# Attention's softmax, query splits and PSUM copies at the scheduler's highest priority, the copies on VectorE, in a hybrid trunk

## The chip, the core and the metric

The kernel runs on one core of a Trainium2 chip. The core has a matrix engine (TensorE, PE in the profile), a vector engine (VectorE, DVE), a scalar engine for functions of one variable (ScalarE, ACT), GpSimd (POOL) and a queue engine from which most transfers are issued (SyncE, SP). Each has its own list of instructions. The metric is the device time of one execution in microseconds (us); of the kernel before there are three, and their median counts.

## The reference: what is computed

Two layers over x (1024 tokens, width 1024, float32). The core of a layer:

```
h    = rms_norm(x, pre_gain) * (1 + scale) + shift      # shift, scale, gate from SiLU(c) @ W_mod + b_mod
proj = h @ w_in                                         # 3088 columns, split among three branches
a_out = sliding_window_attention(rotary(aq), rotary(ak), av, sinks) * silu(ag)
r_out = rms_norm(retention(rq, rk, rv)) * silu(rg)
g_out = rms_norm(gated_linear_attention(gq, gk, gv, log_a)) * silu(gg)
y    = concat(a_out, r_out, g_out) @ w_out
x    = x + gate * rms_norm(y, post_gain)
```

The attention has 8 query heads of width 64 over 2 key/value heads and a window of 128 tokens: token i sees the 128 tokens that end with itself. A learned number for each head, the sink, joins the softmax as one more score and has no value behind it. The three branches have nothing to do with each other until the output projection joins them.

## The kernel before, in words

**Tiles and stages.** The 1024 tokens make 8 tiles of 128. All matrix products of float32 numbers are done in three passes with each operand split into a high and a low part (`PASSES`), so nearly every operand gets a copy (the high part, often on ACT) and a subtraction (the low part, often on DVE). A layer first does the gate paths, retention and the gated linear attention (0 to 340 us and 480 to 820 us of the profiled span), and then attention, which overlaps with the rest of the input projection, the output projection's weights and, in layer 0, the modulation of the next layer (340 to 480 us and 820 to 965 us). The output projection follows.

**What sets the order.** The program is emitted by generators: `job` puts one on a list, `pump` advances all that are due. A generator yields how long the next step should come after (the table `L`, by a planning clock `clk` that counts the matmuls emitted) or a flag for which it waits. PE executes its instructions in exactly the order in which they are emitted, since its order is set by hand (`manual_schedule` for PE). The order of the other engines' instructions is made by a scheduler, by priority among those that can go; unless something else is said, priority is the order of emission. `tc.high_priority()` gives the instructions inside it the highest priority. In the finished program each engine works through its list strictly in order, so that an instruction that waits holds up all that stand behind it. Which engine does an elementwise step is said by the table `EN` ("A" is ACT, "V" DVE, "G" POOL, "S" SP); the helpers `copy` (L150 on ACT, L152 on DVE), `eng`, `dma` (L155), `mult` (L166, matmuls) and `transp` (L181) look there, and so most of the work has the helpers' lines in the profile.

**Attention, tile by tile.** `attn_run` starts `attn_q(l, t)` for t from 0 to 7. For one tile:

1. The queries are split into high and low part by `attn_split` (ACT L912, DVE L913), usually by the tile before.
2. The tile `smx` gets the sink as its last column (DVE L921).
3. 24 matmuls (`aux<-kT,t`) put the scores of this and the previous block of keys into four PSUM banks of the pool `aux`.
4. For t > 0, four copies move the scores of the previous block to `smx` (ACT, `smx<-aux` at L150), and four masked copies put the scores of the own block over them where the mask is set (DVE L947). Since window and block have the same size, one 128x128 square holds both.
5. Softmax: maximum (DVE L949), eight exponentials with sums (ACT L952), reciprocal (DVE L955), product with it (POOL L957).
6. The square is transposed in blocks of 32 (DVE L959). Blocks on the diagonal hold scores of two key blocks; for these, `vd`, the difference of two values (POOL L964), and `pr`, the masked probabilities (POOL L968), are made.
7. The products with the values (`aux<-smx,vx` and those with `vd`) go to four banks `po` of the same pool.
8. **The copies of the change**: four copies of 128x128 bring the result out of PSUM into `ao` (L150, `t<-aux` 128x128; ACT). They are called `aoc0` and `aoc1` in `EN`. Over 2 layers and 8 tiles there are 64.
9. `ao` is stored to DRAM (`aoS<-t`, issued by SP), read back in another arrangement together with the gate (`t<-aoS`, `t<-gS`), multiplied (DVE L1003), split (L152, POOL L1010) and stored to `mixS`, from which `load_mix` reads `mx`, the input of the output projection. In layer 1 `load_mix` belongs to `last_output`.

**PSUM banks.** Of 8 banks, `mm` has three and `aux` five. Scores of a tile take four of `aux`, and so do the products with the values. With the order of PE as emitted, the scores of tile t + 2 go into the banks that the copies of tile t set free: the first score matmul finds one bank free, the second needs the first copy done. Scores of tile t + 2 stand behind the value products of tile t on PE. A buffer is freed when its last reader is done, whichever engine that is.

**Others that the steps touch.** L368 adds up the modulation of the next layer from weights that are being loaded (`st<-in_w_mod_dram`). L575 sums blocks of layer 1's output weights (`st<-in_w_last_dram`). L786 sets `gaT` to zero (POOL). L1276, L1342 and L1408 belong to the output projection. L844 is the low part of the keys. SP issues loads of weights, the stores and read-backs above in one list.

Of the kernel before, what the change touches and what calls it, by code (L numbers as in the profile page):

```python
# [94 lines left out]
def trunk(ctx: ExitStack, tc: tile.TileContext, ins, cst, out):  # L95
    nc = tc.nc
    V, A, G, T = nc.vector, nc.scalar, nc.gpsimd, nc.tensor
# [6 lines left out]
    gp = ctx.enter_context(tc.tile_pool(name="work", bufs=2))  # L104
# [18 lines left out]
    def small(w, dt=F32):  # L123
        return gp.tile([P, w], dt, tag="sm", name=nm("sm"), bufs=BS)
# [20 lines left out]
    def eng(k):  # L145
        return G if EN[k] == "G" else V

    def copy(k, dst, src):
        if EN[k] == "A":
            A.activation(dst, src, AF.Copy)  # L150
        else:
            V.tensor_copy(dst, src)  # L152

    def dma(k, dst, src):
        {"S": nc.sync, "A": A, "P": G}[EN[k]].dma_start(dst, src)  # L155

# [27 lines left out]
    def lat(key, l):  # L184

        return L[key + "@1"] if l and key + "@1" in L else L[key]
# [4 lines left out]
    def flag(name, lat=0.0):  # L191
        flags[name] = clk[0] + lat
# [465 lines left out]
    def pre(l, t, xt, early=False, soon=False):  # L658
# [28 lines left out]
        for j in range(2):  # L687
# [92 lines left out]
    kv = {}  # L780
# [31 lines left out]
    for l in range(DEPTH):  # L812
        c = slice(P * l, P * l + P)
# [93 lines left out]
            job(attn_q(l, t))  # L907

    def attn_split(t):
        qs = [t2(F32R).rearrange("p (k q) -> p k q", k=4) for _ in range(2)]  # L910
        qt = kv[t // 4][:, :, P * (t % 4):P * (t % 4) + P]
        A.activation(qs[0], qt, AF.Copy)  # L912
        eng("qsl").tensor_tensor(qs[1], qt, f(qs[0]), ALU.subtract)  # L913
        kv["qs"][t] = qs

    def attn_q(l, t):

        if t not in kv["qs"]:
            attn_split(t)
        sm = gp.tile([P, 8, 129], F32, tag="smx", name=nm("smx"), bufs=SMB)  # L920
# [16 lines left out]
        if t + 1 < NT and flags.get(("q", l, (t + 1) // 4, 1), 1e9) <= clk[0]:  # L937
            attn_split(t + 1)
        if t % 4 == 3:
            flag(("s", l, t // 4))  # L940
        for g in range(2):
            for r in range(2):
                pv = pss[g][r][:, 0:2 * n].rearrange("p (j c n) -> p j c n", j=2, n=P)
                sv = sm[:, 4 * g + r:4 * g + 4:2, 0:128]
                if t > 0:
                    copy("sprev", sv, pv[:, :, 0, :])
                V.copy_predicated(sv, curmask.unsqueeze(1).to_broadcast((P, 2, P)), pv[:, :, n // P - 1, :])  # L947
        mx = small(8)
        V.tensor_reduce(mx, sm, AX.X, ALU.max, negate=True)  # L949
        sums = small(8)  # L950
        for h in range(8):
            A.activation(sm[:, h, :], sm[:, h, :], AF.Exp, bias=mx[:, h:h + 1],  # L952
                         accum_out=sums[:, h:h + 1])
        rs = small(8)
        V.reciprocal(rs, sums)  # L955
        ph = sm[:, :, 0:128]
        eng("pn").tensor_tensor(ph, ph, rs.unsqueeze(2).to_broadcast((P, 8, P)), ALU.mult)  # L957
        pb = ph.rearrange("p h (j b) -> p h j b", j=4)
        V.transpose(pb, pb)  # L959
        cur, prev = kv[("v", t // 2)], kv.get(("v", max(t - 1, 0) // 2))  # L960
        tc_, tp = t % 2, (t - 1) % 2
        if t > 0:
            vd = gp.tile([P, P], F32, tag="vd", name=nm("vd"), bufs=2)
            G.tensor_tensor(vd, cur[:, 8 + tc_], prev[:, 8 + tp], ALU.subtract)  # L964
            pr = gp.tile([P, 8, 32], F32, tag="pr", name=nm("pr"), bufs=2)
            for i in range(4):
                rr = slice(32 * i, 32 * i + 32)
                eng(f"pr{i}").tensor_tensor(pr[rr], pb[rr, :, i, :], dmask[rr].unsqueeze(1).to_broadcast((32, 8, 32)),  # L968
                                            ALU.mult)
        yield lat("aq4", l)  # L970
        po = [aux() for _ in range(4)]
        for s in range(5 if t else 4):
            for i in range(4):
                rr = slice(32 * i, 32 * i + 32)
                j = (i + s) % 4
# [10 lines left out]
                    mult(d3, w_, x, s == 0, s == (4 if t else -i % 4 if i < 2 else 3), 0.03)  # L986
        ao = t2()
        av = ao.rearrange("p (h q) -> p h q", h=4)
        for i in range(4):
            copy(f"aoc{i % 2}", av[:, :, 32 * i:32 * i + 32], po[i][:, 0:128].rearrange("p (h a) -> p h a", h=4))  # L990
        flag(("av", l, t))
        dma("sao", aoS[t], av)
        if t in (2, 4):
# [5 lines left out]
        av = ao.rearrange("p (k q) -> p k q", k=4)  # L999
# [7 lines left out]
        if not whole or t % 2 == 0:  # L1007
            mh, ml = t2(F32R), t2(F32R)
# [706 lines left out]


B2, B1, BS, BST, MMB, SMB = 10, 8, 11, 5, 3, 3
EN = {"shw0": "V", "shw1": "A", "shw2": "A", "shw3": "A", "slw0": "V", "slw1": "G", "slw2": "V", "slw3": "G", "sht2": "A", "sht3": "A", "sht4": "A", "slt2": "V", "slt3": "G", "slt4": "G", "sd": "V", "mh0": "A", "mh1": "A", "mh2": "A", "mh3": "A", "mf": "A", "ms0": "V", "ms1": "V", "ms2": "V", "ms3": "V", "yg0": "V", "yg1": "V", "ml0": "V", "ml1": "V", "ml2": "V", "ml3": "V", "mod0": "A", "mod1": "V", "qst": "S", "sv": "S", "sg": "S", "lv": "S", "pr0": "G", "pr1": "G", "pr2": "G", "pr3": "G", "smh": "S", "sml": "S", "sm0": "S", "sm1": "S", "lao": "S", "sao": "S", "lmix": "S", "ssg": "S", "lsg": "S", "ssr": "S", "lsr": "S", "lx": "S", "sx": "A", "lw": "S", "lwm": "S", "whi0": "V", "whi1": "A", "whi2": "A", "whi3": "A", "wlo0": "V", "wlo1": "V", "wlo2": "V", "wlo3": "G", "xn0": "V", "xn1": "V", "hlo0": "V", "hlo1": "V", "rot0": "V", "rot1": "V", "rdec": "V", "kslo": "V", "qslo": "V", "vlo": "G", "kT": "A", "qT": "A", "sprev": "A", "pn": "G", "pf0": "A", "aoc0": "A", "aoc1": "A", "qsl": "V", "hng": "V", "mh": "A", "gso": "V", "mg": "V", "mgl": "G", "rT": "A", "rv": "A", "gv": "A", "gk": "A", "ak0": "V", "ak1": "V", "ak2": "V", "ak3": "V", "kd0": "G", "kd1": "G", "kd2": "G", "kx1": "G", "kx2": "G", "kx3": "V", "kx4": "V", "qb": "G", "stx": "V"}
# [44 lines left out]
```

## Time and profile before

| | |
|---|---|
| three executions | 1028.87, 1028.4, 1024.04 us; median 1028.4 |
| the profiled execution, its own time | 1027.32 us |
| its span in the trace | 1025.5 us |
| mean granted PE clock | 0.967 |
| chain that ended last, by engine | PE 65%, DVE 11%, DMA 9%, issue 6%, POOL 5%, ACT 2% |
| data moved by DMA | 163.59 MB, mean 160 GB/s |

How to read the rows. The page gives for each engine the busy time, the share of the span and the number of instructions; PEld is the loading of weights into PE, which runs beside the matmuls. A row of windows has the stretch in us and its length, then busy time and number of instructions of PE, PEld, DVE, ACT and POOL, the granted PE clock as a share of the full one, the busy share of the DMA engines and GB/s. A row of waits names the engine with its instruction, the instruction that ended the wait, and us in total, times and the longest. A row of groups names line, engine, operation, output<-inputs with shapes, the number of instructions, then busy us and mean ns of one, and the engine's idle time before them. A row of the timeline has the start, the duration of a run of like instructions, the engine and line, the number, and in brackets how long the engine was idle before and what ended that. "SPq" is an issue of a transfer by SP. PE's ends are modelled, and a few matmul records are missing (23 of 24 scores in some rows).

### The profile page before, as it was taken

The numbers are of one execution on the slowest core, as the hardware profiler recorded it, in microseconds if no ns is written. First come the engines' busy times: TensorE is split into PE (matmuls) and PEld (weight loads), VectorE is DVE, ScalarE is ACT, GpSimd is POOL, SyncE is SP. The second block draws the span as 40 slices with busy tenths as digits, with TensorE's granted clock in tenths as the row PEclk, the third lists the DMA queues.
The fourth block names the chain that finished last, engine by engine and source line by source line (L and its number), as shares of the span: only waits on it lengthen the run. The fifth ranks groups of instructions, "written<-read, shape, count | busy, mean of one in ns | idle before, by whom it ended". The sixth has DMA issues, their size and how long they took to land.

```text
span 1025.5 us, 21284 instructions
## 1 busy us (share of the span) xinstructions
PE 959.5 (94%) x7965; PEld 832.5 (81%) x7965; DVE 695.7 (68%) x1628; ACT 388.8 (38%) x1152; POOL 282.1 (28%) x319
## 2 busy tenths in 40 slices
PE   5899999999999996888999999999999999778896
PEld 1599999888989775666889999988998877566685
DVE  3789857678666877564388286775774686676776
ACT  2577312333313553412455332133332355454221
POOL 2322111233211355451124101123330044566000
PEclk8899999999999998898999999999999999879899
DMA  8843414433453447867545141351234334787883
GB/s 302 293 132 110 143 43 138 141 104 104 123 175 97 135 139 250 279 191 269 188 151 175 64 155 33 115 175 58 88 104 144 94 111 144 235 278 231 277 255 136
DMA packets 115528, 163.59 MB, mean 160 GB/s; under 512 B 13232, under 2 KB 56796, under 8 KB 115424
## 3 DMA queue, kind: packets, MB, share of 16 engines
q1 hardware_dynamic: 109728, 152.66, 46.9%
q10 hardware_dynamic: 5696, 9.56, 2.5%
q8 instruction: 63, 1.03, 0.4%
q14 instruction: 41, 0.34, 0.1%
HBM read 118.66 MB, written 41.42 MB: 156 GB/s over the span
## 4 chain that ended last, share of the span: by engine, by line
PE 65%; DVE 11%; DMA 9%; issue 6%; POOL 5%; ACT 2%; SPq 1%; ACTq 0%; POOLq 0%; DVEq 0%
PE mm L166 51%; PE aux L166 11%; PE aux L181 3%; DMA aoS<-t 2%; DMA st<-in_w_in_dram 2%; POOL sm L639 1%; DMA t<-gS 1%; POOL smx L957 1%; DMA xk<-in_x_dram 1%; DVE acc L368 1%; ACT smx L952 1%; SPq L155 1%; DMA mx<-mixS 1%; DVE arena L537 1%; POOL pr L968 1%
## 5 line engine op out<-in xcount | busy, mean ns | idle before, releaser
L166 PE MATMUL mm<-arena 128*128 128x256 f32 (+2 forms) x1824 | 296.6, 318 | 2.1 <-ACT arena L708 1.8
L166 PE MATMUL mm<-arena,arena 128*128 128x256 f32 (+2 forms) x1824 | 295.8, 317 | 0.0
L166 PEld LDWEIGHTS mm<-arena 128*128 128x128 f32 x1824 | 257.4, 192 | 24.9 <-ACT arena L708 2.0
L166 PEld LDWEIGHTS mm<-arena,arena 128*128 128x128 f32 x1824 | 254.1, 189 | 23.8 <-issue 2.2
L166 PE MATMUL mm<-arena,mx 128*128 128x512 f32 (+1 forms) x564 | 138.1, 402 | 11.1 <-DMA mx<-mixS 5.9
L639 POOL TENSOR_TENSOR sm<-sm,mhalf 128x1 f32<-128x1 f32 (+1 forms) x64 | 55.3, 864 | 322.5 <-DVE sm L638 309.4
L166 PEld LDWEIGHTS mm<-arena,mx 128*128 128x128 f32 x564 | 106.5, 198 | 37.0 <-issue 7.9
L150 ACT ACTIVATE arena<-st 128x512 fp32r<-128x512 f32 x94 | 55.8, 628 | 64.3 <-PE mm L166 27.0
L537 POOL TENSOR_TENSOR arena<-st,arena 128x512 fp32r<-128x512 f32 x31 | 44.0, 1422 | 120.6 <-ACT arena L150 116.8
L952 ACT ACTIVATE smx<-smx,sm 128x129 f32<-128x129 f32 x128 | 49.7, 390 | 54.6 <-DVE sm L949 54.6
L150 ACT ACTIVATE t<-aux 128x128 f32<-128x128 f32 (+3 forms) x124 | 38.2, 355 | 65.1 <-PE aux L181 63.2
L537 DVE TENSOR_TENSOR arena<-st,arena 128x512 fp32r<-128x512 f32 x77 | 58.1, 776 | 4.0 <-ACT arena L150 2.7
L368 DVE SCALAR_TENSOR_TENSOR acc<-st,c_act,acc 128x512 f32<-128x512 f32 x60 | 47.6, 793 | 16.0 <-DMA st<-in_w_mod_dram 15.4
L957 POOL TENSOR_TENSOR smx<-smx,sm 128x1024 f32<-128x1024 f32 x16 | 32.1, 2004 | 84.2 <-DVE sm L955 71.2
L181 PE MATMUL aux<-c_ident,t 128*128 128x128 f32 (+1 forms) x292 | 48.7, 285 | 6.5 <-DVE t L670 6.2
L968 POOL TENSOR_TENSOR pr<-smx,c_dmask 32x256 f32<-32x256 f32 x56 | 49.6, 886 | 17.1 <-DVE smx L921 7.2
L181 PEld LDWEIGHTS aux<-c_ident,t 128*128 128x128 f32 (+1 forms) x292 | 35.3, 145 | 14.2 <-DVE t L670 8.4
L166 PE MATMUL aux<-kT,t 64*128 64x256 f32 (+1 forms) x384 | 31.7, 308 | 13.9 <-ACT t L150 13.9
L166 PEld LDWEIGHTS aux<-kT,t 64*128 64x128 f32 x384 | 27.4, 205 | 20.1 <-ACT t L150 14.7
L702 ACT ACTIVATE t<-aux,mod,mod 128x128 f32<-128x128 f32 x68 | 25.9, 462 | 44.8 <-DVE t L1311 11.6
L166 PEld LDWEIGHTS aux<-t,mx 32*128 32x128 f32 (+1 forms) x896 | 39.5, 187 | 3.8 <-issue 2.2
L1036 ACT ACTIVATE t<-aux 128x256 f32<-128x256 f32 x32 | 12.3, 384 | 76.9 <-PE aux L166 69.8
(224 smaller groups left out, 1395.3 us busy)
## 6 DMA issues: line engine op xcount, KB each, us to landing
st<-in_w_in_dram SPq DMA_DIRECT2D x96, 256.0 KB, 4.0
st<-in_w_mod_dram SPq DMA_DIRECT2D x64, 256.0 KB, 3.0
mx<-mixS SPq DMA_DIRECT2D x20, 512.0 KB, 5.5
st<-in_w_last_dram SPq DMA_DIRECT2D x36, 256.0 KB, 3.3
mixS<-t SPq DMA_DIRECT2D x64, 128.0 KB, 1.9
mixS<-t SPq DMA_DIRECT2D x26, 256.0 KB, 3.2
wm<-in_w_mod_dram SPq DMA_DIRECT2D x12, 512.0 KB, 5.4
t<-in_x_dram SPq DMA_DIRECT2D x24, 256.0 KB, 4.5
```

The source lines that it names most:

```text
L150: A.activation(dst, src, AF.Copy)
L155: {"S": nc.sync, "A": A, "P": G}[EN[k]].dma_start(dst, src)
L166: T.matmul(dst, lhsT, rhs, start=start, stop=stop)
L181: T.transpose(dst, src, idn)
L368: V.scalar_tensor_tensor(acc, wt, c_act[:, k:k + 1], acc, ALU.mult, ALU.add)
L537: e.tensor_tensor(lo, st, f(hi), ALU.subtract)
L639: G.tensor_tensor(r, r, mhalf[:, :w], ALU.pow)
L702: A.activation(hf[:, ks], at[kt], AF.Identity, scale=gain, bias=shift)
L952: A.activation(sm[:, h, :], sm[:, h, :], AF.Exp, bias=mx[:, h:h + 1], accum_out=sums[:, h:h + 1])
L957: eng("pn").tensor_tensor(ph, ph, rs.unsqueeze(2).to_broadcast((P, 8, P)), ALU.mult)
L968: eng(f"pr{i}").tensor_tensor(pr[rr], pb[rr, :, i, :], dmask[rr].unsqueeze(1).to_broadcast((32, 8, 32)), ALU.mult)
L1036: A.activation(sq, po, AF.Square)
```

## The change

Three things are edited. (1) The softmax part of `attn_q`, from the copies of scores to `vd` and `pr` (steps 4 to 6), becomes a function `soft`, called under `tc.high_priority()`; it hands on `vd` and `pr` in `kv["m"]`. (2) The query split (step 1) and the four copies of step 8 are emitted under `tc.high_priority()` too. (3) These copies go from ACT to VectorE. The order on PE and what is computed stay the same; the sizes of pools and the latencies `L` are not touched. In the built program DVE has 1694 instructions in place of 1630, and ACT 940 in place of 1004.

```diff
     def attn_split(t):
-        qs = [t2(F32R).rearrange("p (k q) -> p k q", k=4) for _ in range(2)]
         qt = kv[t // 4][:, :, P * (t % 4):P * (t % 4) + P]
-        A.activation(qs[0], qt, AF.Copy)
-        eng("qsl").tensor_tensor(qs[1], qt, f(qs[0]), ALU.subtract)
+        with tc.high_priority():
+            qs = [t2(F32R).rearrange("p (k q) -> p k q", k=4) for _ in range(2)]
+            A.activation(qs[0], qt, AF.Copy)
+            eng("qsl").tensor_tensor(qs[1], qt, f(qs[0]), ALU.subtract)
         kv["qs"][t] = qs
+
+    def soft(t, n, pss, sm):
...
+        if t > 0:
+            vd = gp.tile([P, P], F32, tag="vd", name=nm("vd"), bufs=2)
+            G.tensor_tensor(vd, kv[("v", t // 2)][:, 8 + t % 2], kv[("v", (t - 1) // 2)][:, 8 + (t - 1) % 2],
+                            ALU.subtract)
...
+            kv["m"] = vd, pr
 
     def attn_q(l, t):
...
-        cur, prev = kv[("v", t // 2)], kv.get(("v", max(t - 1, 0) // 2))
+        with tc.high_priority():
+            soft(t, n, pss, sm)
+        pb = sm[:, :, 0:128].rearrange("p h (j b) -> p h j b", j=4)
+        cur, prev = kv[("v", t // 2)], kv[("v", max(t - 1, 0) // 2)]
         tc_, tp = t % 2, (t - 1) % 2
...
+        vd, pr = kv["m"] if t else (None, None)
         yield lat("aq4", l)
...
         av = ao.rearrange("p (h q) -> p h q", h=4)
-        for i in range(4):
-            copy(f"aoc{i % 2}", av[:, :, 32 * i:32 * i + 32], po[i][:, 0:128].rearrange("p (h a) -> p h a", h=4))
+        with tc.high_priority():
+            for i in range(4):
+                copy(f"aoc{i % 2}", av[:, :, 32 * i:32 * i + 32], po[i][:, 0:128].rearrange("p (h a) -> p h a", h=4))
...
-EN = { ... "aoc0": "A", "aoc1": "A", ... }
+EN = { ... "aoc0": "V", "aoc1": "V", ... }
```

The lines of `soft` that are left out are those of steps 4 to 6, unchanged in content and order.

More of the change, by code (lines that the diff above doesn't have):

```diff
@@ L909, in attn_split @@
     def attn_split(t):
-        qs = [t2(F32R).rearrange("p (k q) -> p k q", k=4) for _ in range(2)]
         qt = kv[t // 4][:, :, P * (t % 4):P * (t % 4) + P]
-        A.activation(qs[0], qt, AF.Copy)
-        eng("qsl").tensor_tensor(qs[1], qt, f(qs[0]), ALU.subtract)
+        with tc.high_priority():
+            qs = [t2(F32R).rearrange("p (k q) -> p k q", k=4) for _ in range(2)]
+            A.activation(qs[0], qt, AF.Copy)
+            eng("qsl").tensor_tensor(qs[1], qt, f(qs[0]), ALU.subtract)
         kv["qs"][t] = qs
+    def soft(t, n, pss, sm):
+        for g in range(2):
+            for r in range(2):
+                pv = pss[g][r][:, 0:2 * n].rearrange("p (j c n) -> p j c n", j=2, n=P)
+                sv = sm[:, 4 * g + r:4 * g + 4:2, 0:128]
+                if t > 0:
+                    copy("sprev", sv, pv[:, :, 0, :])
+                V.copy_predicated(sv, curmask.unsqueeze(1).to_broadcast((P, 2, P)), pv[:, :, n // P - 1, :])
+        mx = small(8)
+        V.tensor_reduce(mx, sm, AX.X, ALU.max, negate=True)
+        sums = small(8)
+        for h in range(8):
+            A.activation(sm[:, h, :], sm[:, h, :], AF.Exp, bias=mx[:, h:h + 1],
+                         accum_out=sums[:, h:h + 1])
+        rs = small(8)
+        V.reciprocal(rs, sums)
+        ph = sm[:, :, 0:128]
+        eng("pn").tensor_tensor(ph, ph, rs.unsqueeze(2).to_broadcast((P, 8, P)), ALU.mult)
+        pb = ph.rearrange("p h (j b) -> p h j b", j=4)
+        V.transpose(pb, pb)
+        if t > 0:
+            vd = gp.tile([P, P], F32, tag="vd", name=nm("vd"), bufs=2)
+            G.tensor_tensor(vd, kv[("v", t // 2)][:, 8 + t % 2], kv[("v", (t - 1) // 2)][:, 8 + (t - 1) % 2],
+                            ALU.subtract)
+            pr = gp.tile([P, 8, 32], F32, tag="pr", name=nm("pr"), bufs=2)
+            for i in range(4):
+                rr = slice(32 * i, 32 * i + 32)
+                eng(f"pr{i}").tensor_tensor(pr[rr], pb[rr, :, i, :], dmask[rr].unsqueeze(1).to_broadcast((32, 8, 32)),
+                                            ALU.mult)
+            kv["m"] = vd, pr
     def attn_q(l, t):
@@ L940, in attn_q @@
             flag(("s", l, t // 4))
[L941 to L959, printed above, removed]
-        cur, prev = kv[("v", t // 2)], kv.get(("v", max(t - 1, 0) // 2))
-        tc_, tp = t % 2, (t - 1) % 2
[L962 to L965, printed above, removed]
-            for i in range(4):
-                rr = slice(32 * i, 32 * i + 32)
-                eng(f"pr{i}").tensor_tensor(pr[rr], pb[rr, :, i, :], dmask[rr].unsqueeze(1).to_broadcast((32, 8, 32)),
-                                            ALU.mult)
+        with tc.high_priority():
+            soft(t, n, pss, sm)
+        pb = sm[:, :, 0:128].rearrange("p h (j b) -> p h j b", j=4)
+        cur, prev = kv[("v", t // 2)], kv[("v", max(t - 1, 0) // 2)]
+        tc_, tp = t % 2, (t - 1) % 2
+        vd, pr = kv["m"] if t else (None, None)
         yield lat("aq4", l)
@@ L988, in attn_q @@
         av = ao.rearrange("p (h q) -> p h q", h=4)
-        for i in range(4):
-            copy(f"aoc{i % 2}", av[:, :, 32 * i:32 * i + 32], po[i][:, 0:128].rearrange("p (h a) -> p h a", h=4))
+        with tc.high_priority():
+            for i in range(4):
+                copy(f"aoc{i % 2}", av[:, :, 32 * i:32 * i + 32], po[i][:, 0:128].rearrange("p (h a) -> p h a", h=4))
         flag(("av", l, t))
@@ L1717 @@
 B2, B1, BS, BST, MMB, SMB = 10, 8, 11, 5, 3, 3
-EN = {"shw0": "V", "shw1": "A", "shw2": "A", "shw3": "A", "slw0": "V", "slw1": "G", "slw2": "V", "slw3": "G", "sht2": "A", "sht3": "A", "sht4": "A", "slt2": "V", "slt3": "G", "slt4": "G", "sd": "V", "mh0": "A", "mh1": "A", "mh2": "A", "mh3": "A", "mf": "A", "ms0": "V", "ms1": "V", "ms2": "V", "ms3": "V", "yg0": "V", "yg1": "V", "ml0": "V", "ml1": "V", "ml2": "V", "ml3": "V", "mod0": "A", "mod1": "V", "qst": "S", "sv": "S", "sg": "S", "lv": "S", "pr0": "G", "pr1": "G", "pr2": "G", "pr3": "G", "smh": "S", "sml": "S", "sm0": "S", "sm1": "S", "lao": "S", "sao": "S", "lmix": "S", "ssg": "S", "lsg": "S", "ssr": "S", "lsr": "S", "lx": "S", "sx": "A", "lw": "S", "lwm": "S", "whi0": "V", "whi1": "A", "whi2": "A", "whi3": "A", "wlo0": "V", "wlo1": "V", "wlo2": "V", "wlo3": "G", "xn0": "V", "xn1": "V", "hlo0": "V", "hlo1": "V", "rot0": "V", "rot1": "V", "rdec": "V", "kslo": "V", "qslo": "V", "vlo": "G", "kT": "A", "qT": "A", "sprev": "A", "pn": "G", "pf0": "A", "aoc0": "A", "aoc1": "A", "qsl": "V", "hng": "V", "mh": "A", "gso": "V", "mg": "V", "mgl": "G", "rT": "A", "rv": "A", "gv": "A", "gk": "A", "ak0": "V", "ak1": "V", "ak2": "V", "ak3": "V", "kd0": "G", "kd1": "G", "kd2": "G", "kx1": "G", "kx2": "G", "kx3": "V", "kx4": "V", "qb": "G", "stx": "V"}
@@ new lines @@
+EN = {"shw0": "V", "shw1": "A", "shw2": "A", "shw3": "A", "slw0": "V", "slw1": "G", "slw2": "V", "slw3": "G", "sht2": "A", "sht3": "A", "sht4": "A", "slt2": "V", "slt3": "G", "slt4": "G", "sd": "V", "mh0": "A", "mh1": "A", "mh2": "A", "mh3": "A", "mf": "A", "ms0": "V", "ms1": "V", "ms2": "V", "ms3": "V", "yg0": "V", "yg1": "V", "ml0": "V", "ml1": "V", "ml2": "V", "ml3": "V", "mod0": "A", "mod1": "V", "qst": "S", "sv": "S", "sg": "S", "lv": "S", "pr0": "G", "pr1": "G", "pr2": "G", "pr3": "G", "smh": "S", "sml": "S", "sm0": "S", "sm1": "S", "lao": "S", "sao": "S", "lmix": "S", "ssg": "S", "lsg": "S", "ssr": "S", "lsr": "S", "lx": "S", "sx": "A", "lw": "S", "lwm": "S", "whi0": "V", "whi1": "A", "whi2": "A", "whi3": "A", "wlo0": "V", "wlo1": "V", "wlo2": "V", "wlo3": "G", "xn0": "V", "xn1": "V", "hlo0": "V", "hlo1": "V", "rot0": "V", "rot1": "V", "rdec": "V", "kslo": "V", "qslo": "V", "vlo": "G", "kT": "A", "qT": "A", "sprev": "A", "pn": "G", "pf0": "A", "aoc0": "V", "aoc1": "V", "qsl": "V", "hng": "V", "mh": "A", "gso": "V", "mg": "V", "mgl": "G", "rT": "A", "rv": "A", "gv": "A", "gk": "A", "ak0": "V", "ak1": "V", "ak2": "V", "ak3": "V", "kd0": "G", "kd1": "G", "kd2": "G", "kx1": "G", "kx2": "G", "kx3": "V", "kx4": "V", "qb": "G", "stx": "V"}
```

## The prediction

> **What bounds the kernel now.** I read the head of the page first, then busy time by stage, then PE's waits.
>
> ```profile
> span 1025.5 us, 21284 instructions
> PE 959.5 (94%) x7965; PEld 832.5 (81%) x7965; DVE 695.7 (68%) x1628; ACT 388.8 (38%) x1152; POOL 282.1 (28%) x319
> ```
> ```profile
> core 0: us, PE busy (x) PEld busy (x) DVE busy (x) ACT busy (x) POOL busy (x), PEclk, DMA share, GB/s
> 340.00:480.00 140.00, 120.91 (x1131) 95.09 (x1130) 89.75 (x140) 55.83 (x212) 62.50 (x57) 0.93 0.66 207
> 480.00:820.00 340.00, 337.60 (x2784) 309.92 (x2783) 219.21 (x605) 123.23 (x341) 66.06 (x89) 1.00 0.38 123
> 820.00:965.00 145.00, 125.25 (x1151) 98.41 (x1150) 101.33 (x153) 68.22 (x232) 72.92 (x63) 0.90 0.65 203
> 878.00:900.00 22.00, 16.12 (x141) 12.48 (x141) 14.51 (x22) 8.25 (x31) 10.85 (x11) 0.77 0.81 273
> ```
> ```profile
> PE aux L166 <- ACT t L150: 17.7, 7, 6.4
> PE aux L166 <- DVE smx L947: 10.5, 3, 5.3
> PE mm L166 <- DMA mx<-mixS: 5.9, 2, 5.2
> ```
> TensorE is busy for 94% of the span, and its instruction order is fixed by hand. The two attention stages (340 to 480 and 820 to 965 us) are the ones that the change touches. PE idles there for 19.1 and 19.8 us, in the middle of layer 1 for 2.4 us only. The attention waits are named: 17.7 us in 7 waits for the copies of values out of PSUM (ACT, L150), 10.5 us in 3 for softmax (L947). DVE is busy for 64% and 70% of these stages, ACT for 40% and 47%. So the change aims at a real wait, and moves the copies from the emptier engine to the fuller one. What decides is where in DVE's order they stand.
>
> **The change part by part.** *Price of the copies.*
>
> ```profile
> L150 ACT ACTIVATE t<-aux 128x128 f32<-128x128 f32 x64 | 12.8, 268 | 1.7 <-DVE t L1311 1.7
> L844 DVE TENSOR_TENSOR kT<-aux,kT 128x128 fp32r<-128x128 f32 x16 | 4.5, 282 | 0.5 <-ACT kT L843 0.2
> ```
> ```profile
> 354.47 1.43 DVE L947 COPY_PREDICATED smx<-c_curmask,aux 128x256 f32<-128x256 int32 x4
> ```
> ACT loses 64 copies of 268 ns (12.8 us, overlapped). DVE gains 64. No row shows a plain 128x128 copy on DVE; the nearest is L844, of the same size out of PSUM, at 282 ns: 18 us at most. Four in a row lie between ACT's own 0.74 us (row 360.78 below) and four masked copies of twice the size in 1.43; I take 0.8, nearer to the first. [...]
>
> *Priority.* In the built programs PE's order is the same. Softmax and splits move by few places on ACT, DVE and POOL (two swaps on POOL), since most stood as early as their inputs allow: I cost that at nothing beyond the places named below. What counts is that each engine executes in order, so the copies now wait for what stands before them on DVE. I go through them by tile.
>
> *Layer 0, tile 1: a new wait.*
>
> ```profile
> 360.78 0.74 ACT L150 ACTIVATE t<-aux 128x128 f32<-128x128 f32 x4
> ```
> ```profile
> 363.96 1.70 PE L166 MATMUL aux<-kT,t 64*128 64x256 f32 x24
> 396.51 2.31 PE L166 MATMUL aux<-kT,t 64*128 64x256 f32 x23 [3.59 <-ACT t L150]
> 428.40 2.92 PE L166 MATMUL aux<-kT,t 64*128 64x256 f32 x23 [3.33 <-ACT t L150]
> 465.03 6.79 PE L166 MATMUL mm<-arena,mx 128*128 128x512 f32 x20 [5.25 <-DMA mx<-mixS]
> ```
> ```profile
> 363.11 1.25 DVE L959 STREAM_TRANSPOSE smx<-smx 128x1024 f32<-128x1024 f32 x1
> ...
> 364.85 0.82 DVE L368 SCALAR_TENSOR_TENSOR acc<-st,c_act,acc 128x512 f32<-128x512 f32 x1
> 365.59 0.66 DVE L921 COPY smx<-sink 128x8 f32<-128x8 f32 x1
> ...
> 367.45 1.44 DVE L947 COPY_PREDICATED smx<-c_curmask,aux 128x256 f32<-128x256 int32 x4
> ...
> 397.69 0.66 DVE L921 COPY smx<-sink 128x8 f32<-128x8 f32 x1
> ...
> 418.98 1.25 DVE L959 STREAM_TRANSPOSE smx<-smx 128x1024 f32<-128x1024 f32 x1 [2.01 <-POOL smx L957]
> ...
> 424.88 1.23 DVE L921 COPY smx<-sink 128x8 f32<-128x8 f32 x1
> 432.50 0.69 DVE L1003 SCALAR_TENSOR_TENSOR t<-t,t 128x512 f32<-128x512 f32 x1 [6.39 <-DMA t<-gS]
> ```
> ACT made tile 1's copies at 360.78, well before PE's scores of tile 3 at 363.96, which need their banks and did not wait. In the new order they stand on DVE behind the transpose, L368 and the sink of tile 2: first end at 365.59 + 0.66 + 0.3 = 366.6, plus up to 0.65 because tile 0's copies are also on DVE by then. PE stalls 2.6 to 3.2 us. The masked copies of tile 3 (367.45) slip 1.5, tile 2's own copies add 0.8: +2.3.
>
> *Tiles 3 and 4.* At 396.51 PE waits for ACT's copies; now they follow the sink at 397.69, first end 398.65 instead of about 396.5: +2.
>
> ```profile
> 418.17 0.40 SPq L155 DMA_DIRECT2D aoS<-t  x1
> ...
> 423.17 0.34 SPq L155 DMA_DIRECT2D t<-aoS  x1
> ...
> 427.84 0.32 SPq L155 DMA_DIRECT2D t<-gS  x1
> ```
> Tile 4's copies stand behind the transpose that waits for POOL until 418.98: done at about 421, so the store aoS, issued at 418.17, goes at 421 or later. Behind it on SP's queue stand the read-back (423.17), gS and t<-gS (427.84), for which L1003 at 432.50 waits: +2.9, with the +2.3 carried +5.1. POOL's work behind L1003 and softmax of tile 6 follow.
>
> *Gains, tiles 5 to 7.* The wait before 428.40 (3.33) shrinks: on DVE the copies follow the sink, free at 424.88 + 1.23 = 426.1, two before ACT's. SP issues moved ahead at tiles 6 and 7 give about 1 us. PE then waits 5.25 for the load of mx at 465.03; stalls of PE before it end in this slack, late stores do not. Net of the layer, +2.5 (bounds 0, when the slack takes all, and 2.9 + 2 - 2 + 2.9 = +5.8).
>
> *Layer 1.*
>
> ```profile
> 851.42 1.70 PE L166 MATMUL aux<-kT,t 64*128 64x256 f32 x24
> ...
> 874.16 3.98 PE L166 MATMUL mm<-arena,arena 128*128 128x512 f32 x16
> ...
> 879.07 1.69 PE L166 MATMUL aux<-kT,t 64*128 64x256 f32 x23 [0.62 <-ACT t L150]
> ...
> 892.15 2.75 PE L166 MATMUL aux<-smx,vx 32*64 32x128 f32 x58 [5.27 <-DVE smx L947]
> ...
> 895.47 5.74 PE L166 MATMUL mm<-arena 128*128 128x512 f32 x16
> ...
> 916.85 2.93 PE L166 MATMUL aux<-kT,t 64*128 64x256 f32 x23 [6.35 <-ACT t L150]
> ...
> 962.34 5.42 PE L166 MATMUL mm<-arena,mx 128*128 128x512 f32 x12 [4.40 <-DVE t L1408]
> ```
> ```profile
> 854.79 0.31 DVE L921 COPY smx<-sink 128x8 f32<-128x8 f32 x1
> 855.98 1.15 DVE L575 TENSOR_TENSOR st<-st,st 128x512 f32<-128x512 f32 x1 [0.88 <-DMA st<-in_w_last_dram]
> ...
> 886.08 0.69 DVE L1003 SCALAR_TENSOR_TENSOR t<-t,t 128x512 f32<-128x512 f32 x1 [3.82 <-DMA t<-gS]
> ...
> 915.28 0.69 DVE L575 TENSOR_TENSOR st<-st,st 128x512 f32<-128x512 f32 x1
> ```
> Tile 1: its copies follow the sink at 854.79, first end 854.79 + 0.31 + 0.3 = 855.4; scores of tile 3 had no wait at 851.42: a new stall of 4.0. Softmax of tile 3 stands behind L575, which waits for a DMA in any case, so only tile 4 is late, by 1.3 (the 2.3 of layer 0 less about 1 of that cover, an estimate). Tile 3: its copies stand behind L1003, which waits for t<-gS until 886.08. PE's scores of tile 5, at 879.07 now, can go on from 886.08 + 0.69 + 0.3 = 887.1, and with L1003 itself late by the 1.3 to 2.3 found so far from about 889: an 8 us stall. It largely takes the place of the 5.27 before 892.15, since PE's 6.1 us between 880.8 and 886.9 come after it: to 895.2 at least, 3 to 5 late. Tile 5: copies follow L575, from 915.97, first end 916.3, half a microsecond before 916.85; the 6.35 there takes up PE's 3 to 5, so that only softmax's delay remains, +2.3. At the end four copies stand in the DVE run that PE waits for (4.40 before 962.34): +0.75. Net +3 (bounds 0 and 4.0 + 5 + 0.75 = +9.75).
>
> *The clock.* The row 878 to 900 has a granted clock of 0.77, and 16 matmuls take 5.74 us at 895.47, behind the idle 5.27, against 3.98 at 874.16: 1.8 us behind a long idle. The 24 scores take 1.70 without a wait and 2.92 behind 3.33, so 1.2 behind a middling one. I count nothing more for it, since old stalls of that kind go as new ones come. [...]
>
> **Sum.** 2.5 + 3 = +5.5 on the profiled execution, whose time is 1027.3 (span 1025.5 and 1.8 around it): 1032.8. The median is 1028.4, 1.1 higher: 1033.9, say 1034.
>
> **The rivals.**
> 1. *ACT's relief wins (faster).* Its place is PE's 17.7 us of waits for L150. DVE gives -2 at 428.40 and -0.5 at 916.85, SP's order -1, and a shorter queue on ACT for exp up to 0.74 per late tile, say -1 in all: -4.5, 1024. It decides if the stalls at 363.96 and 851.42 end wholly in the waits of 5.25 and 6.35, that is, if softmax of tiles 3 and 4 slips by under 1 us. For it: those slacks. Against it: masked copies stand right behind the stalled scores.
> 2. *It moves waits, no more.* PE's stalls take the place of others and the stores' delay is hidden behind the DMAs already waited for: 0, 1028 to 1029. For it: 5.25 and 5.27. Against: tile 4's late store is itself on the DMA's path.
> 3. *Nothing is absorbed.* 2.9 + 2 + 4 + 8 - 3 = +14: 1042. Against: a stall of 8 and one of 5.27 in the same place overlap.
> 4. *Half clock behind the new stalls.* 1.2 to 1.8 behind each of the two of 4 and 8 us: +3 on the forecast, 1037. For it: the row at 895.47. Against: there a slow stretch exists already.
> That the priority does nothing by itself is contained in the forecast: all terms are of the copies.
>
> **How the numbers follow.** Forecast 0.42 (own range 1029 to 1040), relief 0.16, moved waits 0.22, nothing absorbed 0.12, half clock 0.08. The measurement can tell 0.5% (5.1 us) from no change, so the bounds are 1023.3 and 1033.5. Slower: 0.25 of the forecast's 0.42 (six tenths of its own range lie above 1033.5), with 0.12 and 0.08: 0.45. Faster: the rival on 1024 spreads to both sides of the bound, and a gain in places not seen belongs to it: 0.16. Same: the rest, 0.39. The range 1023 to 1042 leaves out half of rival 1 and half of rival 3, 0.14.
>
> **What would show it.** Right: scores of tile 3 in layer 0 show a wait of about 3 us for a DVE copy; in layer 1 one of about 4, and scores of tile 5 a wait of about 8 that ends on DVE; aoS of tile 4 is issued 3 us later; DVE gains 13 to 18 us busy, ACT loses 13. Wrong: if the list of waits shows less than 17.7 us for the copies on DVE and softmax starts no later from tile to tile, relief has won; if mx is waited for 5 us longer at 465, the stores' delay is worth more than I gave it.

## The result, and the profile after

The kernel with the change takes 1032.72 us, median of 14 executions (1029.83 to 1035.72), the kernel before 1027.62 (1024.04 to 1030.88): a ratio of 1.0054, 95% interval 1.004 to 1.0068, or 5.1 us slower.

The profile after was taken in an execution of 1029.83 us, the fastest of its 14, the one before in one of 1027.32. So the two traces lie 2.5 us apart and show half of the loss. What single executions can't tell was measured by timed variants below. The head of the page of the kernel after, and its busy time in the five stages (same columns as before; lines of `soft` and all that follow carry other numbers now: L921 is L954, L947 is L925, L959 is L937, L1003 is L1014, L1408 is L1419):

```profile
span 1028.0 us, 21277 instructions
PE 963.1 (94%) x7965; PEld 835.0 (81%) x7965; DVE 707.5 (69%) x1692; ACT 379.1 (37%) x1088; POOL 279.7 (27%) x319
```
```profile
340.00:480.00 140.00, 127.54 (x1133) 99.37 (x1132) 92.67 (x171) 49.15 (x176) 59.87 (x56) 0.90 0.63 202
820.00:965.00 145.00, 120.83 (x1145) 95.40 (x1145) 108.17 (x180) 63.00 (x198) 71.45 (x62) 0.92 0.63 199
```

DVE gained 11.8 us, ACT lost 9.7. The stage of layer 1 lost 4.4 us of PE's busy time to idling; the stage of layer 0 has more busy PE time than before, a part of it at a lower clock (0.90 against 0.93). The waits of PE after, longest in sum first:

```profile
PE aux L166 <- DVE t L152: 22.7, 7, 6.2
...
PE aux L166 <- DVE smx L925: 2.8, 3, 1.1
PE aux L166 <- DVE smx L937: 2.7, 1, 2.7
PE aux L166 <- ACT t L150: 2.6, 2, 1.5
...
PE mm L166 <- DMA mx<-mixS: 1.6, 3, 0.9
```

The waits for the copies were 17.7 us on ACT. They are 22.7 on DVE, with 2.6 left for ACT's other copies. In turn the waits for the masked copies (L947, now L925) fell from 10.5 to 2.8 and those for mx from 5.9 to 1.6: much of the new idling stands where old idling was. The places on PE, with what ended the wait in brackets:

```profile
366.45 2.92 PE L166 MATMUL aux<-kT,t 64*128 64x256 f32 x23 [2.81 <-DVE t L152]
...
400.43 2.93 PE L166 MATMUL aux<-kT,t 64*128 64x256 f32 x23 [2.72 <-DVE t L152]
...
466.52 3.07 PE L166 MATMUL mm<-arena,mx 128*128 128x512 f32 x12 [0.22 <-DMA mx<-mixS]
```
```profile
856.14 2.92 PE L166 MATMUL aux<-kT,t 64*128 64x256 f32 x23 [4.11 <-DVE t L152]
...
889.94 2.92 PE L166 MATMUL aux<-kT,t 64*128 64x256 f32 x23 [5.08 <-DVE t L152]
...
921.37 2.92 PE L166 MATMUL aux<-kT,t 64*128 64x256 f32 x23 [6.18 <-DVE t L152]
...
964.84 5.42 PE L166 MATMUL mm<-arena,mx 128*128 128x512 f32 x12 [5.94 <-DVE t L1419]
```

DVE's order around the first of them and around the two in layer 1 (start, duration, instruction):

```profile
363.09 1.25 DVE L937 STREAM_TRANSPOSE smx<-smx 128x1024 f32<-128x1024 f32 x1
...
364.83 0.81 DVE L368 SCALAR_TENSOR_TENSOR acc<-st,c_act,acc 128x512 f32<-128x512 f32 x1
365.57 0.64 DVE L954 COPY smx<-sink 128x8 f32<-128x8 f32 x1
366.12 0.87 DVE L152 COPY t<-aux 128x128 f32<-128x128 f32 x4
```
```profile
855.62 0.29 DVE L954 COPY smx<-sink 128x8 f32<-128x8 f32 x1
855.81 0.67 DVE L152 COPY t<-aux 128x128 f32<-128x128 f32 x3
...
888.99 0.69 DVE L1014 SCALAR_TENSOR_TENSOR t<-t,t 128x512 f32<-128x512 f32 x1 [4.39 <-DMA t<-gS]
889.60 0.88 DVE L152 COPY t<-aux 128x128 f32<-128x128 f32 x4
...
920.08 1.03 DVE L575 TENSOR_TENSOR st<-st,st 128x512 f32<-128x512 f32 x1 [2.54 <-DMA st<-in_w_last_dram]
921.03 0.87 DVE L152 COPY t<-aux 128x128 f32<-128x128 f32 x4
```

Each of these four stalls ends with the first copy, and each copy starts the moment that DVE is done with what stands ahead: a transpose, a sum and the sink, a product that waits for a read-back, a sum that waits for a load of weights. Four copies take 0.87 us.

### The profile page after: what moved, and what is told of

Same layout as the page of the kernel before. It is cut to its first block, busy times and chain, and to the rows that moved or that the text cites. A ratio compares the mean times of both kernels' runs of the same rounds, so it can differ in the third digit from the quotient of the medians.

```text
span 1028.0 us, 21277 instructions
## 1 busy us (share of the span) xinstructions
PE 963.1 (94%) x7965; PEld 835.0 (81%) x7965; DVE 707.5 (69%) x1692; ACT 379.1 (37%) x1088; POOL 279.7 (27%) x319
## 5 line engine op out<-in xcount | busy, mean ns | idle before, releaser
L166 PEld LDWEIGHTS mm<-arena 128*128 128x128 f32 x1824 | 257.6, 192 | 24.9 <-ACT arena L708 2.0
L166 PEld LDWEIGHTS mm<-arena,arena 128*128 128x128 f32 x1824 | 256.0, 190 | 24.8 <-issue 2.4
L166 PE MATMUL mm<-arena,mx 128*128 128x512 f32 (+1 forms) x564 | 135.8, 398 | 7.5 <-DVE t L1419 5.9
L150 ACT ACTIVATE arena<-st 128x512 fp32r<-128x512 f32 x94 | 55.9, 628 | 75.2 <-PE mm L166 34.0
L166 PE MATMUL aux<-kT,t 64*128 64x256 f32 (+1 forms) x384 | 37.6, 339 | 21.8 <-DVE t L152 21.8
L166 PEld LDWEIGHTS aux<-kT,t 64*128 64x128 f32 x384 | 32.3, 236 | 28.9 <-DVE t L152 23.4
L945 POOL TENSOR_TENSOR pr<-smx,c_dmask 32x256 f32<-32x256 f32 x56 | 46.8, 835 | 18.2 <-DVE smx L937 12.1
L150 ACT ACTIVATE t<-aux 128x256 fp32r<-128x256 f32 (+2 forms) x60 | 25.4, 447 | 63.5 <-PE aux L181 63.2
L166 PE MATMUL aux<-t,mx 32*128 32x32 f32 (+1 forms) x896 | 40.7, 272 | 0.0
```

Source lines behind the costliest of these rows:

```text
L166: T.matmul(dst, lhsT, rhs, start=start, stop=stop)
```

## The experiments

Every variant was timed in five rounds beside the kernel before, on its chip (12 executions each, 6 of `e2_eng` and `p2_recip_behind`); the ratio is against that kernel. Where a count of microseconds is given for a ratio, it is the ratio times 1026, the median of before in those runs (1025.5 to 1026.1).

**The change taken apart.** Two variants do one half each, and two do it in one layer. `e1_prio` keeps the priority and puts the copies back on ACT:

```diff
-EN = { ... "aoc0": "V", "aoc1": "V", ... }
+EN = { ... "aoc0": "A", "aoc1": "A", ... }
```

> Copies back on ACT, priority kept. Theory A (all of the +5.1 us comes from where the copies stand on DVE): within 1.5 us of the kernel before, PE waits for ACT copies of about 17 us again. Rival B (the priority costs by itself, by what it moves on POOL and SP): +3 us or more. Rival C (priority alone would gain, and the change hides it): -2 us or less.

Measured: 0.9987 (0.9968 to 1.0007), with 18.1 us of waits for ACT's copies in its trace. Rival B is out, and rival C is not shown: -1.3 us with an interval that reaches from -3.3 to +0.7.

`e2_eng` has the copies on DVE, and no priority:

```diff
-        with tc.high_priority():
+        with ExitStack():        # at all three places
```

> Copies on DVE, no priority anywhere. Theory A: the whole of the change, +5 us, within 1.5, against before, and PE waits for L152 of about 23 us. Rival B: under +2 us. Rival C: over +7 us.

Measured: 1.0078 (1.0058 to 1.0097), +8 us, with 24.9 us of waits for the copies. By the median that is rival C; the interval (6.0 to 9.9 us) also reaches into theory A's 3.5 to 6.5. All of the loss, and more, is in the move to DVE. That exceeds the change's own 1.0054, whose interval it overlaps, so the priority may give back 1 to 3 us; neither run proves it alone. In its built program DVE's order differs from the change's in small ways, such as which of a tile's copies and a query split goes first.

`e3_l0` and `e4_l1` have the priority, and the copies on DVE in one layer:

```diff
-                copy(f"aoc{i % 2}", av[...
+                copy("aoc0" if l == 0 else "aoc1", av[...      # e4_l1: l == 1; aoc0 "V", aoc1 "A"
```

> Only layer 0's 32 copies on DVE, priority kept. As forecast: +2.5 us. By the profiles of before and after (layer 1 begins at the same time in both): 0, within 1 us, with the wait for mx near 465 us shortened from 5.25 to under 2 us.

> Only layer 1's 32 copies on DVE, priority kept. As forecast: +3 us, with a stall of about 4 before the scores of tile 3 and of 5 to 8 before those of tile 5. If layer 0 costs nothing: the whole +5, and e3_l0 nothing.

Measured: layer 0 1.0013 (0.9998 to 1.0028), layer 1 1.0041 (1.0026 to 1.0055): +1.3 and +4.2 us against before, or +2.7 and +5.5 against `e1_prio`. Layer 1 costs most; its stalls before the scores of tiles 3 and 5 are 4.09 and 4.82 us in e4, where about 4 and 5 to 8 were expected. Layer 0 costs little, between the forecast's 2.5 and the nothing that the pair of traces seemed to show. The traces can't decide on layer 0: up to its end `x1` and `x3` (below) have the same copies on the same engines, and yet the same matmuls of layer 1 begin 4.4 us apart in them. First x1's row, then x3's:

```profile
552.54 1.04 PE L181 MATMUL aux<-c_ident,t 128*128 128x128 f32 x8
```
```profile
556.95 1.04 PE L181 MATMUL aux<-c_ident,t 128*128 128x128 f32 x8
```

**Single stalls of layer 1.** Only tile 1's, or only tile 3's copies on DVE:

```diff
+                copy("aoc0" if (l, t) == (1, 1) else "aoc1", av[...      # x3: (1, 3)
```

> Only the four copies of layer 1's tile 1 on DVE, priority kept, all others on ACT. Theory A with the profiles of before and after: this one stall of 4 us moves all of layer 1, +3 to +4 us against the copies all on ACT. If the loss adds up of many tiles, or of DVE's busy time: under +1.

> Only the four copies of layer 1's tile 3 on DVE, priority kept. As forecast: a stall of 8 us before the scores of tile 5 in place of the one of 5.27 before the values of tile 4, +3 to +5 us at that place, of which the wait of 6.4 before the scores of tile 7 takes up nearly all: under +1.5 in the end. If it isn't taken up: +3 or more.

Measured: tile 1 1.0007 (0.9992 to 1.0021), tile 3 0.9992 (0.9972 to 1.0012). Against `e1_prio` that is +2.1 and +0.5 us, with wide intervals, where all of layer 1's copies cost +5.5. Neither of these two stalls carries the layer: against before, both intervals end below the 2.7 us at which layer 1's begins. The expectation for tile 1 was too high. Tile 3 alone on DVE shows what the forecast said of it:

```profile
890.45 2.92 PE L166 MATMUL aux<-kT,t 64*128 64x256 f32 x23 [8.62 <-DVE t L152]
...
919.81 2.93 PE L166 MATMUL aux<-kT,t 64*128 64x256 f32 x23 [6.14 <-ACT t L150]
```

The stall of 8.6 us is there, the one of 5.27 before the values of tile 4 is gone, and the time is the same within the interval. In the full change this stall shows as 5.08: counted from the scores of tile 1 (824.56 in the change, 827.14 in x3), PE comes to it 5.6 us later, held up by the stall for tile 1, and the copies come 2.1 us later. It ends at 889.94, where DVE's chain puts it.

**Load or place?** `d1_load_only` loads DVE without a PSUM bank that waits for the added work: copies on ACT, and a reduction of each copied tile on DVE, whose result nothing uses.

```diff
+    scr = cp.tile([P, 4], F32, name="scr")
...
+        with tc.high_priority():
+            V.tensor_reduce(scr, ao.rearrange("p (h q) -> p h q", h=4), AX.X, ALU.add)
```

> Copies on ACT, priority kept, and on DVE an extra reduction of the copied tile (128x512, out of SBUF, its result is not used) for each of the 16 tiles: about 0.65 us each by half of the 1.22 us of the reduction over 1032, 10 us of DVE in all, at about the places where the change has its copies, but no PSUM bank waits for it. Theory A (the banks' wait at that place is the cost): within 1.5 us of the priority alone, so 0.997 to 1.001 of the kernel before. Rival D (DVE's load delays softmax and so all): +3 us or more over the priority alone, 1.002 or more.

```profile
L1005 DVE TENSOR_REDUCE scr<-t 128x4 f32<-128x512 f32 x16 | 10.8, 675 | 2.6 <-ACT t L150 2.6
```

Measured: 10.8 us more on DVE for 1.0005 (0.9988 to 1.0022), that is +1.8 us against `e1_prio`, where the change with 14.2 us of copies is +6.9. That is between the two outcomes of the expectation (under 1.5 and over 3). The load may be a part of the cost, a quarter by the medians of these ratios; with these intervals anything from nothing to about 4.5 us is possible. It is not the whole: against before, this interval ends at 1.0022 and the change's begins at 1.004.

**Other places on DVE.** An order (no wait) between the copies and one instruction of the next tile's softmax; `behind` is called both behind that instruction and behind the copies, whichever is emitted last:

```diff
+    def behind(t):
+        a, b = kv.get(("tr", t)), kv.get(("cp", t - 1))
+        if a is not None and b is not None:
+            tc.add_manual_dep(a.ins, b.ins.name, mybir.DependencyInfo(
+                mybir.DependencyClass.NoSync, mybir.DependencyReason.DATA), reason="issue_after")
...
-        V.transpose(pb, pb)
+        kv["tr", t] = V.transpose(pb, pb)        # p2: V.reciprocal(rs, sums)
+        behind(t)
```

> All 64 copies on DVE with priority, as in the change, but the transpose of the next tile is made to stand behind them in DVE's order (an order only, no wait). Theory A, place: most of the loss of 5.1 us goes, within 2 us of the kernel before, and the stall of 4 us before layer 1's scores of tile 3 falls under 2. Rival D, engine (16 us more on DVE cost what they cost wherever they stand): +4 to +6 us stays.

> The same one step earlier: the reciprocal of the next tile's softmax stands behind the copies. Theory A: at most +1 us, or faster than the kernel before by up to 3 us, since DVE idled about 2 us ahead of that reciprocal and the copies could end ahead of where ACT made them. Rival D: +4 to +6 us. A third outcome, softmax held up by the copies: +3 us or more with the stalls before the scores gone and waits for softmax in their place.

Measured: copies ahead of the transpose 1.0021 (1.0001 to 1.004), ahead of the reciprocal 1.0068 (1.0042 to 1.0093). The same 64 copies on the same engine cost 2 us or 7 by the order on DVE, so load alone doesn't set the cost. Theory A's first number came out by the median (+2.2 us), but not the stall that was to fall under 2: it is 2.92 in p1, and PE's waits for the copies add up to 25.6 us there, above the 22.7 of the change. So p1's gain is not in the sum of these waits. Theory A's second number failed: further ahead was worse, and no better than the change itself. DVE around tile 1 of layer 1, first with the copies ahead of the transpose, then ahead of the reciprocal (L574 is L575, L960 the sink, L938 the reciprocal, L942 and L943 the transpose, L151 the copies):

```profile
849.59 0.20 DVE L938 RECIPROCAL sm<-sm 128x8 f32<-128x8 f32 x1 [2.07 <-ACT smx L935]
850.57 1.74 DVE L574 TENSOR_TENSOR st<-st,st 128x512 f32<-128x512 f32 x1 [0.78 <-DMA st<-in_w_last_dram]
...
852.91 0.67 DVE L151 COPY t<-aux 128x128 f32<-128x128 f32 x3
...
854.31 1.22 DVE L942 STREAM_TRANSPOSE smx<-smx 128x1024 f32<-128x1024 f32 x1
```
```profile
851.94 0.69 DVE L574 TENSOR_TENSOR st<-st,st 128x512 f32<-128x512 f32 x1 [1.59 <-DMA st<-in_w_last_dram]
852.55 0.17 DVE L960 COPY smx<-sink 128x8 f32<-128x8 f32 x1
852.62 0.68 DVE L151 COPY t<-aux 128x128 f32<-128x128 f32 x3
...
854.02 0.19 DVE L938 RECIPROCAL sm<-sm 128x8 f32<-128x8 f32 x1
...
856.72 1.23 DVE L943 STREAM_TRANSPOSE smx<-smx 128x1024 f32<-128x1024 f32 x1
```

In both, the copies stand behind a sum of weights (L574) that waits for its load, and start at 852.9 and 852.6. The stricter order did not bring them forward; it put the reciprocal behind them, from 849.59 to 854.02, and softmax with it. The time is that of the third outcome of the expectation, but the stalls did not go: in p2's trace PE waits 22.8 us in 8 waits for the copies, and 5.3 for the masked copies where the change has 2.8. That trace is of the fastest of six executions (1029.59 us, median 1032.68), so what the loss of 7 us is made of is not shown.

At tile 5 of layer 1, p1's order does put the copies ahead of the sum of weights (they start at 914.56, the sum at 920.92 after 4.34 us of waiting for its load). The scores of tile 7 have no wait there, where the change has 6.18, and the next wait, for tile 6's copies behind another sum that waits for its load (1.09 us), is 8.31. Copies ahead of these sums at every tile were not tried.

**Is there a better version?** Three variants with the priority. `b1_two_on_dve` has tile 5's copies of both layers on DVE with the transpose behind them, and all others on ACT (the condition as above with `(l, t) in ((0, 5), (1, 5))`). `b3_exp_behind` has all copies on ACT, and the next tile's eight exponentials behind them in ACT's order; `b4_exp_behind_some` does so for tiles 3 and 5 only:

```diff
-            A.activation(sm[:, h, :], sm[:, h, :], AF.Exp, ...
+            e = A.activation(sm[:, h, :], sm[:, h, :], AF.Exp, ...
+            kv.setdefault(("ex", t), []).append(e)
+        behind(t)                # the order is made for each of the eight
```

> Copies on DVE for tile 5 of both layers alone, with the next transpose behind them; all others on ACT, priority kept. These are the places where PE waited for ACT 2.2 and 7.0 us and with the copies ahead of the transpose 0.6 us and not at all. Theory A: the wait of 7.0 before the scores of tile 7 in layer 1 goes; -1 to -3 us against the kernel before, if what follows there (the load of mx, the copies of tile 6) doesn't end later all the same. Rival: the wait moves to tile 6's copies, as it did with all copies ahead of the transpose (8.3 us there): 0.

> Copies on ACT, priority kept, and the eight exponentials of the next tile are made to stand behind them in ACT's order. Theory A (what counts is what stands ahead of the copies, on either engine): PE's waits for L150 fall from 18 us to under 8, and the time by 1 to 4 us against the kernel before, unless softmax is late by as much. Rival: exponentials that wait for PE's value products hold up softmax: waits for the masked copies grow from 9.5 us, +2 us or more.

> The same for four places alone, tiles 3 and 5 of both layers, where PE waited for ACT 4.4, 0.9, 2.2 and 7.0 us. Theory A: -1 to -3 us against the kernel before. Rival: the waits move to the next ones: within 1 us.

Measured: 0.9985 (0.9965 to 1.0005), 0.9987 (0.9971 to 1.0003) and 1.0043 (1.0022 to 1.0065). The first two are no better than `e1_prio` (0.9987) and not certainly faster than the kernel before. b4 is 4 us slower, which neither of its outcomes had; its waits for L150 rose to 24.8 us. In b3 the waits for L150 did fall, to 3.5 us, and those for softmax rose to 19.7 (its L944 is the transpose, which ends softmax):

```profile
PE aux L165 <- DVE smx L944: 19.7, 5, 6.7
...
PE aux L165 <- ACT t L150: 3.5, 3, 1.4
```

The waits were exchanged. What stands behind the long one at tile 5 of layer 1, which b1 and b4 were meant to remove, is seen in `e1_prio`, where ACT makes these copies, and in b1, where DVE does (its L574 and L602 are L575 and L603). ACT and DVE in e1, then DVE in b1:

```profile
915.45 0.63 ACT L150 ACTIVATE arena<-st 128x512 fp32r<-128x512 f32 x1 [4.36 <-DVE st L575]
915.99 0.26 ACT L150 ACTIVATE t<-aux 128x128 f32<-128x128 f32 x1
```
```profile
912.86 1.25 DVE L937 STREAM_TRANSPOSE smx<-smx 128x1024 f32<-128x1024 f32 x1 [1.04 <-POOL smx L935]
914.31 1.10 DVE L575 TENSOR_TENSOR st<-st,st 128x512 f32<-128x512 f32 x1 [0.21 <-DMA st<-in_w_last_dram]
```
```profile
914.47 0.69 DVE L574 TENSOR_TENSOR st<-st,st 128x512 f32<-128x512 f32 x1 [2.41 <-DMA st<-in_w_last_dram]
915.25 0.69 DVE L602 TENSOR_TENSOR st<-st,st 128x512 f32<-128x512 f32 x1
915.86 0.88 DVE L151 COPY t<-aux 128x128 f32<-128x128 f32 x4
```

ACT had been idle for 4.36 us ahead of the copies: they stand behind the high part of the output weights, which needs the sum L575. That sum stands behind the next tile's transpose on DVE and needs a load; the transpose ends 0.2 us before the load is there, so that both hold it. In b1 the copies and the sum stand ahead of the transpose, and the load alone holds them: the sum still starts at 914.47, and PE waits 6.60. In b4 the sum waited 8.37 us for the load, to 915.31, and PE 9.66 for the copies. So on either engine the wait of 6 to 7 us is not that of the engine that copies: without the load it would have been at most 0.2 us shorter in e1, and without the transpose it stayed in b1. The expectations of b1 and b4 had read it as ACT's own, and were wrong in that.

## Why the prediction was right, and where it was not

- **Total.** +5.5 forecast, +5.1 measured, and the reason given is borne out as far as the runs go: priority alone costs nothing (e1), the move alone +8 (+6 to +10, e2), and another order of the same copies on DVE +2 (p1). That the sum came so near is in part luck: it adds 2.5 for layer 0 and 3 for layer 1, where the runs have +1.3 and +4.2, so that the two misses (each within its interval) cancel.
- **Price of the copies.** Forecast 0.8 us for four, measured 0.87, and 14.2 us for the 64 (L152), under the upper bound of 18. Right. The totals of the engines moved by less than the prediction's sign said (DVE +11.8 for 13 to 18, ACT -9.7 for 13), since other instructions changed too.
- **Layer 0, tile 1.** Forecast: the first copy behind the sink at 366.6, a stall of 2.6 to 3.2. Measured: sink at 365.57, copies at 366.12, stall 2.81. Right.
- **Tiles 3 and 4 of layer 0.** Forecast for the scores of tile 5: +2, with +2.3 carried; they moved from 396.51 to 400.43, +3.9. Forecast for the store of tile 4: at 421 or later, and L1003 late by 2.9 to 5.1. The trace has 423.14 for the store, 5.0 later and not the 3 of the prediction's sign, and L1003 (L1014) from 432.50 to 435.92, +3.4:

```profile
423.14 0.34 SPq L155 DMA_DIRECT2D aoS<-t  x1
...
431.11 0.32 SPq L155 DMA_DIRECT2D t<-gS  x1
```

- **Net of layer 0.** Forecast +2.5, measured +1.3 (-0.2 to +2.9) against before and +2.7 against e1. The forecast stands within the intervals, its upper bound of 5.8 is out, its lower one of 0 isn't. The wait for mx of 5.25 shrank to 0.22, as its part as slack demands.
- **Layer 1, tiles 1 and 3.** Stall of 4.0 forecast, 4.11 measured. For tile 3, 8 us forecast that end at about 889; it ends at 889.94, shows 5.08 behind the first stall, and 8.62 by itself. Right in place and mechanism.
- **The clock.** The step "I count nothing more for it, since old stalls of that kind go as new ones come" failed at one place and held for the layer. The stretch of PE from 846 to 873 us, before and after:

```profile
846.00:873.00 27.00, 27.00 (x309) 21.29 (x315) 18.25 (x28) 14.27 (x56) 12.72 (x14) 1.00 0.47 137
```
```profile
846.00:873.00 27.00, 22.89 (x269) 18.11 (x268) 18.13 (x35) 12.21 (x47) 10.83 (x11) 0.87 0.43 130
```
```profile
859.00 2.04 PE L166 MATMUL mm<-arena 128*128 128x512 f32 x4
```

  PE had neither a wait nor a lowered clock there before (1.00); now it has both. Behind the stall of 4.11 the scores take 2.92 us instead of 1.70, and the next four matmuls 2.04 (row above) instead of 1.19 in the trace of before: 2 us more, so that this stall costs about 6 and not 4. The granted clock is 0.50 while these scores run (856.14 to 859.00). Later in layer 1 old slow stretches do go. Between the same matmuls of PE, from the scores of tile 1 to the wait for L1408, before and after:

```profile
824.70:962.30 137.60, 117.89 (x1125) 92.72 (x1124) 96.12 (x143) 65.34 (x227) 69.58 (x61) 0.91 0.67 209
```
```profile
824.56:964.80 140.24, 116.12 (x1125) 91.81 (x1124) 104.89 (x176) 61.12 (x195) 68.75 (x61) 0.92 0.65 205
```

  PE is busy 1.8 us less in sum and idle 4.4 more, +2.6 in this pair. About 6.5 us are lost up to the scores of tile 5, where the stall for tile 1 lies, and 3.9 come back behind them, all of it in PE's busy time. The fourth rival had the mechanism and the amount (1.2 to 1.8 for a stall) nearly right, for this one place. In before the granted clock was 0.50 in three such places too: behind the 3.33 (428.40 to 431.32), the 5.27 (892.15 to 894.90) and the 6.35 us (916.85 to 919.78). What it did behind other waits stands in the last section.
- **Net of layer 1.** Forecast +3, measured +4.2 (2.7 to 5.6), so the net stands near the lower end of the interval. A step of it failed: "the 6.35 there takes up PE's 3 to 5". It takes up nothing: the wait is 6.18 and ends 4.5 us later, at 921.37 instead of 916.85. I had put the copies of tile 5 at 915.97, behind L575 as it stood before, and not asked what sets L575. SP's rows, before first and then after, show it:

```profile
902.22 0.32 SPq L155 DMA_DIRECT2D aoS<-t  x1
...
907.90 1.28 SPq L155 DMA_DIRECT2D st<-in_w_last_dram  x2
```
```profile
907.24 0.34 SPq L155 DMA_DIRECT2D aoS<-t  x1
...
911.96 0.43 SPq L155 DMA_DIRECT2D st<-in_w_last_dram  x1
```

  The store of tile 4's result is 5.0 us late, since its copies are; loads of weights queue behind it on SP and are 4.1 late; L575 waits for one (2.54 us, to 920.08), and the copies of tile 5 wait behind L575. DVE itself comes to L575 at 917.54, 2.3 us later than before, so that this path makes about half of the 4.5. So the delay of one tile's copies comes round to a later one through SP. I had followed exactly this path in layer 0 and left it out in layer 1. The trace of `e4_l1` shows it too (store at 904.65, load at 909.62, L575 at 918.34 after a wait of 3.38, a stall of 6.69), but no run cut it, and what the difference of 1.2 us between forecast and measurement consists of stays open.
- **The end.** +0.75 forecast for four copies ahead of the wait for L1408; that wait grew from 4.40 to 5.94, but PE stands only 2.5 us later there, after 4.5 at 921: some 2 us were given back in between. They are in PE's busy time (38.35 us before, from 910.12 to 962.30, and 35.94 after, from 914.80 to 964.80, at a granted clock of 0.85 and 0.92); its idle time there is about the same (13.8 and 14.1). The forecast has nothing of that.
- **Rivals.** Relief of ACT (1024) is out: the longest wait that was booked to ACT was a load's and a transpose's, and on DVE the sum of these waits grew. Moved waits alone (1028 to 1029) are out by the interval. Of 14 us if nothing were absorbed, 5 came. The half clock in full (+3 on top, 1037) is out too: over the whole stage the granted clock of layer 1 rose from 0.90 to 0.92, and that of layer 0 fell from 0.93 to 0.90.

What stays open: how the +5.1 us divides exactly among layer 0, layer 1 and the priority (each interval is 3 to 4 us wide), how much of it is DVE's load (0 to about 4.5 us by d1), why p1 costs less and p2 more, and whether copies ahead of the weights' sums at every tile would make DVE the better place.

## What to carry to other kernels

Before work is moved to another engine, find its place in that engine's order and ask what each instruction ahead of it waits for: here the copies that free a buffer inherited the waits of what stood before them (at tile 5 of layer 1 the 2.54 us that L575 waited for its load, to 920.08; the copies began at 921.03). Highest priority did not lift the copies over such waits here, and alone it changed the time by less than the interval. A wait that the profile books to the copying engine may belong to a load or another engine further up, as the 6.97 us booked to ACT at tile 5 of layer 1 in `e1_prio` did; follow what stands ahead of the releaser before counting on the wait as slack or as gain. And where single executions scatter by 6 to 7 us, as here, a pair of traces shows mechanisms, and timed variants show the size.

## What the runs showed that was not expected

- Stalls of 2.72 and 2.81 us in the change were followed by a granted clock of 0.50: the 23 scores behind them took 2.93 and 2.92 us, as long and at the same clock as behind 5.08 and 6.18. Behind 0.88 us (a row of after at 906.07) they took 1.70, at 1.00. The length of the stall alone does not decide: behind 2.17 us they took 2.93 (e1, at 429.53), behind 2.15 us 1.70 (p2, at 904.27), and behind 3.60 us 1.77 (b4, at 878.89).
- Executions of one kernel scatter by 6 to 7 us (1024.0 to 1030.9 before, 1029.8 to 1035.7 after), more than the whole effect.
